# A Fourier and state-space block: which engine makes the second parts of the projection's weights while a context or first latent scan runs

## The chip, the cores and the metric

The kernel runs on one core of a Trainium2 chip, in one launch. The metric is the device time of that launch in microseconds (us), lower is better. Five engines of the core take part, each with its own list of instructions that it works off in order, and each waiting for the others through semaphores:

- TensorE (PE in the profile): matmuls; its weight loads (PEld) overlap them.
- VectorE (DVE), ScalarE (ACT) and GpSimd (POOL): element-wise work.
- SyncE (SP): issues nearly all DMAs. A few are issued by ScalarE.

The engines share an on-chip memory (SBUF). Matmuls write to PSUM, a small second memory, from which VectorE and ScalarE read.

## The reference, cut to what matters

One layer: a normed and modulated input is projected. The projected columns u go through a 2-D Fourier transform. x, B and C go through a row convolution and then a chunked scan in two directions. z is a gate. The context tokens (256) go the same way first, without an output: only their final scan states are kept, and the latent scans (2048 tokens) start from them.

```python
def mixer_inputs(h, w_in, conv_w, conv_b, rows, row_len, full):
    p = h @ (w_in if full else w_in[:, XBC_OFF:])
    ...
    xbc = jax.nn.silu(conv_rows(rest[..., :CONV_DIM], conv_w, conv_b, rows, row_len))
    dt_raw = rest[..., CONV_DIM:]
...
    y_c, hf_c, hb_c = ssd_bidir(xs_c, B_c, C_c, dt_c, dt_bias[l], a_log[l], h0, h0, keep_ctx)
...
    u_f, z_x, xs_x, B_x, C_x, dt_x = mixer_inputs(hx, w_in[l], conv_w[l], conv_b[l], rows, GRID_W, True)
    y_x, _, _ = ssd_bidir(xs_x, B_x, C_x, dt_x, dt_bias[l], a_log[l], hf_c, hb_c, True)
    x = x + gm_x * rms_norm(mixer_output(uf_x, z_x, xs_x, y_x, d_skip[l], g_ssd[l], w_out[l]), g_post_mix[l])
    ...
    x = x + gf_x * rms_norm(swiglu(hx2, w_gate[l], w_up[l], w_down[l]), g_post_ffn[l])
```

The scan's step, for each chunk of 128 tokens, is h = exp(a) h + s, where s is a matmul of B with weighted x.

## The kernel before, in words

**Exact products.** Every large product is made of three fast ones. A float32 operand is split into a first part `hi` (rounded) and a second part `lo` = value - hi; the product is hi·hi + hi·lo + lo·hi. For weights this is `wparts` (L217): the 512 KB block `raw` of 128 columns is loaded by SP, `hi` is a cast on ScalarE, and `lo` a subtraction of two SBUF tiles of 128x1024, by default on VectorE (V), or on the engine that the caller names. `hi` and `lo` have two buffers each; the four `raw` buffers are shared with the blocks `adaw` of the modulation's weights.

**Projection.** The tokens are in three sections: 2 is the context (256 tokens), 0 and 1 are the halves of the latent ones (1024 each). `blocks` (L789 to L801) lists the column blocks in their order. Blocks of section 2 and 0 alternate first, for B and x, and share weights. Then come the four C blocks of section 0, and then section 1: two u, four B, six x, and C and z blocks mixed. A block (`project`, L439) is 16 steps (`project_step`, 8 for each 512 tokens) of three matmuls into PSUM. There are three PSUM places for blocks: two named `mm` and one named `y`. Between, the 24 columns of dt make a section of their own (`dt_section`, L454): matmuls named `w48` or `w`, then a chain of some 25 small VectorE operations on `dtp`, with two sums by matmul (`a<-dtp,kc` and `a<-dtp,ones`), three exponentials and a logarithm on ScalarE.

**After a block** `finish_block` (L1552) starts two chains of work: `split` (L819), which makes `hi` and `lo` of the block after the next, and `column_block` (L576). The latter is, for x, B and C, one ScalarE and six VectorE operations (`acc`, the convolution, reading PSUM), a SiLU on ScalarE, and for x and B transposes by TensorE and a store. The PSUM place is free again when the sixth VectorE operation is done. Blocks of section 0 beside the context have their `lo` on VectorE (`brief`), all others after the first on GpSimd.

**Scans.** `scan_steps` (L655) runs the context's scan (`scan[2]`), then the forward scan over section 0 (`scan[0]`) and over section 1 (`scan[1]`). A chunk is: load x and B rows (`l_x`, `l_b`), weight x on GpSimd (`xd`, which has one buffer), decay the state on GpSimd (`h`), four matmuls `a<-xd,l_b`, and two VectorE additions that free the two small PSUM banks `a`. `scan[2]` has four such steps.

**Section 1's inputs** (`section_chain`): its second half of rows `xt` is squared (ScalarE), scaled by rows (VectorE, `xt<-xt,rq_y`), transposed by TensorE (32 transposes `a<-ident,xt`), modulated (ScalarE, `v`) and split into `actA` hi and lo by VectorE and GpSimd. The second halves of the two u blocks wait for it.

**The Fourier steps** (`fourier_steps`, L709) run beside section 1's blocks, on VectorE above all, and wait where VectorE is planned to be late (`spare`, L686).

**The order.** All this is issued in one order, written by a planner (`Pace`, L72): chains of work are generators; each issued operation is charged an estimated cost on its engine (L142 to L158), and a chain's next step is taken when the planned TensorE time has come to it. So a change of an operation's engine changes the planned times, and with them the order of later instructions on every engine. `ada_steps` (VectorE's `adacc`) fills in where a block is at its sixth step.

After the last projected block come 16 chunks of outputs and the feed-forward network, which is most of the program.

Of the kernel before, what the change touches and what calls it, by code (L numbers as in the profile page):

```python
# [164 lines left out]
def fourier_ssd_block(ctx, tc, a):  # L165
    nc = tc.nc
    pace = Pace()
    V, S, G, T = (Paced(e, n, pace) for e, n in
                  ((nc.vector, "DVE"), (nc.scalar, "ACT"), (nc.gpsimd, "POOL"), (nc.tensor, "PE")))
# [47 lines left out]
    def wparts(raw, shape, engine=V, first=None, pool=wp, tags=("hi", "lo")):  # L217
        hi = pool.tile(shape, F32R, tag=tags[0], name="hi")
        (first.tensor_copy if first else S.copy)(hi, raw)
        lo = pool.tile(shape, F32R, tag=tags[1], name="lo")  # L220
        engine.tensor_tensor(lo, raw, hi.bitcast(F32), op=ALU.subtract)
        return hi, lo
# [353 lines left out]
    def column_block(kind, j, sec, ps, done):  # L576

        n = CTX if sec == 2 else HALF
        row = CTX if sec == 2 else ROW
        res = []  # L580
        if kind == "x":
            yield from conv(ps, n, row, j, res, done)
            yield from to_tokens(res[0], n, xtok_d[sec], j)
        elif kind == "B":
            yield from conv(ps, n, row, XB + j, res, done)
            if sec < 2:
                put(bT_d[sec][j], res[0])
            yield from to_tokens(res[0], n, btok_d[sec], j)
        elif kind == "C":
            yield from conv(ps, n, row, XB + BB + j, res, done)  # L590
            put(cT_d[sec][j], res[0])
        elif kind == "z":
            sz = g_.tile([P, HALF], F32, tag="tok", name="sz")
            S.activation(sz, ps, AF.Silu)
            done()
            put(szT_d[sec][j], sz)
            last_sz[:] = [sz]
        elif kind == "u":
            uf = g_.tile([P, HALF], F32, tag="tok", name="uf")
            S.copy(uf, ps)  # L600
            done()
            put(ufT_d[sec][j], uf)
# [186 lines left out]
    def group(kind, sec):  # L789
        return [(kind, j, sec) for j in range({"z": ZB, "u": 2, "x": XB, "B": BB, "C": CB}[kind])]  # L790
# [3 lines left out]
    blocks = group("z", 0)[:4] + [("dt", 0, 2)]  # L794
# [15 lines left out]
    def shared(bi):  # L810
        return bi > 0 and blocks[bi - 1][0] != "dt" and blocks[bi] == (*blocks[bi - 1][:2], 0) and blocks[bi - 1][2] == 2
# [7 lines left out]
    def split(bi, *engines, **where):  # L819
        if bi < len(blocks) and shared(bi):  # L820
            wq[bi] = wq[bi - 1]
        elif bi in wraw:
            wq[bi] = wparts(wraw.pop(bi), [P, KD, P], *engines, **where)
        yield
# [580 lines left out]
    with tc.manual_schedule(engines=ordered):  # L1405
# [115 lines left out]
        chains, splits, scan, prep1, begun = {}, {}, {}, {}, {}  # L1521
# [4 lines left out]
        def after(bi, n):  # L1526

            i = nth[bi] + n
            return plain[i] if i < len(plain) else nblk
# [24 lines left out]
        def finish_block(bi, ps):  # L1554
            kind, j, sec = blocks[bi]
            live = [chains[b] for b in plain if b in chains and not chains[b].done and (blocks[b][2] == 2) == (sec == 2)]
            pace.drain(*live[:-1])
            two = after(bi, 2)
            brief = two < nblk and any(blocks[b][2] == 2 for b in (after(bi, 1), two))
            splits[two] = pace.start(split(two, *((V, V) if brief and blocks[two][2] != 2 else (V,) if brief else (G,))))  # L1560
            chains[bi] = pace.start(column_block(kind, j, sec, ps.rearrange("p a b -> p (a b)"), lambda: read.add(bi)))

        def late_steps():
# [9 lines left out]
        while bi < nblk:  # L1573
# [17 lines left out]
            if bi == first1:  # L1591
                b1 = after(bi, 1)
                want(after(bi, 3))
                pz = [place(bi), place(b1)]
                pace.drain(splits[b1])
                for i, b in ((0, bi), (0, b1), (1, bi), (1, b1)):
                    if i == 1 and b == bi:
                        pace.drain(prep1[1])
                    for k in range(KD):
                        project_step(pz[b - bi], wq[b], acts[1][i], i, k)  # L1600
                        pace.due()
                    if i == 1:
                        finish_block(b, pz[b - bi])
                fnet = pace.start(when(lambda: settled("u", 1), fourier_steps()))
                late.append(pace.start(when(lambda: fnet.done and ada.done, load_wo(0, "B"))))
                bi += 2
                continue
# [22 lines left out]
            else:  # L1630
                ps = project(bi, wq[bi], acts[sec])
            finish_block(bi, ps)
            if kind == "x" and j == XB - 1:
                scan[sec] = pace.start(when(lambda sec=sec: ready_to_scan(sec), scan_steps(sec)), 8.0)
# [372 lines left out]
```

## Time and profile before

| | |
|---|---|
| runs timed | 2349.7, 2342.34 and 2350.42 us, median 2349.7 |
| the profiled execution | 2342.21 us, of which 2340.4 are its span |
| mean granted TensorE clock | 0.988 |
| first to last move of this change's weights | 291 to 489 us from the span's start |
| last projected block's end | 704 us |

How to read it: a line of a timeline has the start and the duration in us, the engine, the line in the program (nearly all instructions have L143, the helper that issues them), the operation, the tiles out<-in, and in brackets how long the engine stood idle before it and what released it. DVE stands for VectorE, POOL for GpSimd, ACT for ScalarE, and SPq is the queue from which SyncE issues DMAs. Where an operation's duration is longer than that of its equals, it was held up after its start. A window's row has its start and end, its length, the busy time of PE, PEld, DVE, ACT and POOL (each with its count of instructions), then the mean granted clock of TensorE, the share of the DMA engines and GB/s.

### The profile page before, as it was taken

The page shows a single profiled execution, that of the slowest core. Times are in us where ns is not written, and L with a number is a line of the kernel's source. Part 1 is how long each engine was busy: PE and PEld are TensorE (multiplying, and loading weights), DVE is VectorE, ACT ScalarE, POOL GpSimd, SP SyncE. Part 2 cuts the span into 40 slices and gives each one's busy share as a digit, 9 for nine tenths or more (in the row PEclk, how much of TensorE's full clock was granted, in tenths as well). Part 3 has the DMA queues.
Part 4 walks back from the last instruction along what each step waited for, and adds up shares of the span by engine and source line. Part 5 has one row for each costly group of instructions (what it writes and reads, how often), then busy time and mean ns, then how long its engine had stood idle before and what let it go on. Part 6 is the DMA issues. An engine that isn't in the chain of part 4 may idle for free. (4 is left out here: it accounts for less than half of the span.)

```text
span 2340.4 us, 29917 instructions
## 1 busy us (share of the span) xinstructions
PE 2254.8 (96%) x10861; PEld 1850.9 (79%) x10861; DVE 1543.2 (66%) x2248; ACT 1050.4 (45%) x1949; POOL 871.9 (37%) x595
## 2 busy tenths in 40 slices
PE   7999988999999999988999999999999999999998
PEld 3888866878888888866888887788888878888786
DVE  3475667796548888876655556855555565769666
ACT  4433324344347787756433324333333335454444
POOL 2200133522333444434555554355555541500501
PEclk9999999999999999999999999999999999999999
DMA  9354354554767888733333332532333364458343
GB/s 304 115 164 135 104 169 128 183 170 145 262 209 240 256 253 252 239 113 117 113 108 99 104 99 100 166 113 95 108 99 104 109 230 147 152 178 300 90 134 114
DMA packets 261890, 369.77 MB, mean 158 GB/s; under 512 B 16920, under 2 KB 179812, under 8 KB 258927
## 3 DMA queue, kind: packets, MB, share of 16 engines
q1 hardware_dynamic: 232086, 337.08, 45.2%
q10 hardware_dynamic: 29656, 30.78, 3.8%
q8 instruction: 86, 1.41, 0.3%
q14 instruction: 62, 0.50, 0.1%
HBM read 273.09 MB, written 94.72 MB: 157 GB/s over the span
## 5 line engine op out<-in xcount | busy, mean ns | idle before, releaser
L143 PE MATMUL b<-wd,hd 128*128 128x512 f32 x1848 | 423.1, 391 | 4.4 <-ACT hd L143 2.2
L143 PEld LDWEIGHTS b<-wd,hd 128*128 128x128 f32 x1848 | 347.4, 188 | 80.0 <-DVE slot L143 4.1
L143 PE MATMUL mm<-slot,wa 128*128 128x512 f32 x1584 | 378.8, 392 | 10.5 <-ACT sg L143 6.9
L143 PEld LDWEIGHTS mm<-slot,wa 128*128 128x128 f32 x1584 | 297.7, 189 | 75.8 <-ACT sg L143 7.7
L143 PE MATMUL mm<-actC,wa 128*128 128x512 f32 x984 | 241.5, 394 | 7.3 <-DVE u L143 7.2
L143 POOL TENSOR_TENSOR ws<-raw 128x512 f32<-128x512 f32 x88 | 127.2, 1446 | 310.1 <-DMA raw<-in_w_up_dram 116.5
L143 PE MATMUL mm<-actB,wa 128*128 128x512 f32 x1020 | 239.4, 390 | 0.0
L143 PEld LDWEIGHTS mm<-actC,wa 128*128 128x128 f32 x984 | 186.6, 190 | 47.6 <-issue 8.7
L143 POOL TENSOR_TENSOR lo<-raw,hi 128x1024 fp32r<-128x1024 f32 x33 | 80.1, 2428 | 384.9 <-ACT hi L143 374.3
L143 PEld LDWEIGHTS mm<-actB,wa 128*128 128x128 f32 x1020 | 191.2, 188 | 39.6
L143 ACT CAST wa<-ws 128x512 fp32r<-128x512 f32 x176 | 109.1, 621 | 252.2 <-PE mm L143 212.2
L143 DVE TENSOR_TENSOR wa<-ws,wa 128x512 fp32r<-128x512 f32 x176 | 156.0, 888 | 59.0 <-ACT wa L143 56.1
L143 DVE SCALAR_TENSOR_TENSOR acc<-mm,convw,acc 128x1008 f32<-128x1008 f32 (+3 forms) x156 | 161.9, 1040 | 34.3 <-ACT acc L143 31.6
L143 PE MATMUL mm<-actA,hi 128*128 128x512 f32 x512 | 164.8, 402 | 2.9 <-DVE actA L143 2.5
L143 POOL TENSOR_TENSOR rq_y<-rq_ms,mhalf 128x1 f32<-128x1 f32 (+2 forms) x60 | 42.3, 710 | 331.0 <-DVE rq_ms L143 324.1
L143 DVE TENSOR_TENSOR u<-u,mm 128x512 f32<-128x512 f32 x126 | 86.5, 687 | 116.3 <-PE mm L143 116.2
L143 DVE TENSOR_TENSOR wa<-raw,wa 128x512 fp32r<-128x512 f32 x132 | 120.3, 912 | 65.0 <-ACT wa L143 64.6
L143 ACT CAST wa<-raw 128x512 fp32r<-128x512 f32 x132 | 82.3, 624 | 162.2 <-PE mm L143 147.7
L143 ACT ACTIVATE ab<-ab,lda 128x128 f32<-128x128 f32 x384 | 118.8, 390 | 0.4 <-ACT sz L143 0.4
L143 DVE TENSOR_TENSOR hd<-hraw,hd 128x512 fp32r<-128x512 f32 x154 | 110.0, 715 | 6.2 <-ACT hd L143 6.1
L143 PEld LDWEIGHTS mm<-actA,hi 128*128 128x128 f32 x512 | 93.7, 190 | 24.8 <-DVE actA L143 3.2
L143 PE MATMUL mm<-actC,hi 128*128 128x512 f32 (+1 forms) x384 | 108.0, 368 | 0.0
(306 smaller groups left out, 4329.1 us busy)
## 6 DMA issues: line engine op xcount, KB each, us to landing
hraw<-hg SPq DMA_DIRECT2D x70, 512.0 KB
ab<-acsd SPq DMA_DIRECT2D x128, 192.0 KB
raw<-in_w_in_dram SPq DMA_DIRECT2D x44, 512.0 KB
raw<-in_w_gate_dram SPq DMA_DIRECT2D x44, 512.0 KB
raw<-in_w_up_dram SPq DMA_DIRECT2D x44, 512.0 KB
hg<-hs SPq DMA_DIRECT2D x22, 1024.0 KB
adaw<-in_w_ada_dram SPq DMA_DIRECT2D x32, 512.0 KB
l_x<-xtok SPq DMA_DIRECT2D x33, 384.0 KB
```

The costliest lines, as they stand in the source:

```text
L143: r = issue(out, *args, **kw)
```

## The change

```diff
@@ -1557,7 +1557,8 @@
             pace.drain(*live[:-1])
             two = after(bi, 2)
             brief = two < nblk and any(blocks[b][2] == 2 for b in (after(bi, 1), two))
-            splits[two] = pace.start(split(two, *((V, V) if brief and blocks[two][2] != 2 else (V,) if brief else (G,))))
+            busy = any(not scan[k].done for k in scan if k != 1)
+            splits[two] = pace.start(split(two, *((V, V) if brief and blocks[two][2] != 2 else (V,) if brief or busy else (G,))))
             chains[bi] = pace.start(column_block(kind, j, sec, ps.rearrange("p a b -> p (a b)"), lambda: read.add(bi)))
```

`scan[2]` and `scan[0]` are in the list from the time that the last x block of their section is finished in the planner. From then until `scan[0]` is done in the plan, the `lo` of each new block is issued on VectorE. These are eleven: those of C1 to C3 of section 0, and of section 1 both u blocks, all four B blocks and the first two x blocks. On GpSimd eleven rows are gone, on VectorE there are eleven more. No arithmetic changes. The rest of the order moves by the planner, up to the last projected block; behind it nothing does.

The first place is GpSimd's list beside the context's scan, from the `lo` of C2 on (`xd` are the weighted x of the scan's steps, `actC` second parts of section 1's first inputs). Before:

```order
L143 TENSOR_TENSOR rq_y_2402<-rq_ms_2381,mhalf_86 128x4
L143 TENSOR_TENSOR lo_2437<-raw_2334,hi_2435 128x1024
L143 TENSOR_TENSOR xd_2441<-l_x_2390,scs_127 128x768
L143 TENSOR_TENSOR actC_2462<-v_2477,actC_2461 128x512
L143 TENSOR_TENSOR xd_2504<-l_x_2394,scs_127 128x768
L143 TENSOR_TENSOR actC_2462<-v_2511,actC_2461 128x512
L143 TENSOR_TENSOR h_2444<-h_2443,hdec_128 128x768
L143 TENSOR_TENSOR actC_2462<-v_2555,actC_2461 128x512
L143 TENSOR_TENSOR xd_2585<-l_x_2394,scs_127 128x768
L143 TENSOR_TENSOR actC_2462<-v_2592,actC_2461 128x512
L143 TENSOR_TENSOR lo_2624<-raw_2429,hi_2622 128x1024
L143 TENSOR_TENSOR xd_2634<-l_x_2390,scs_127 128x768
```

And now:

```order
L143 TENSOR_TENSOR rq_y_2405<-rq_ms_2381,mhalf_86 128x4
L143 TENSOR_TENSOR xd_2441<-l_x_2390,scs_127 128x768
L143 TENSOR_TENSOR xd_2464<-l_x_2394,scs_127 128x768
L143 TENSOR_TENSOR actC_2472<-v_2487,actC_2471 128x512
L143 TENSOR_TENSOR h_2444<-h_2443,hdec_128 128x768
L143 TENSOR_TENSOR actC_2472<-v_2512,actC_2471 128x512
L143 TENSOR_TENSOR xd_2553<-l_x_2394,scs_127 128x768
L143 TENSOR_TENSOR actC_2472<-v_2570,actC_2471 128x512
L143 TENSOR_TENSOR actC_2472<-v_2591,actC_2471 128x512
L143 TENSOR_TENSOR xd_2604<-l_x_2390,scs_127 128x768
```

The `lo` of C2, ahead of the first `xd`, and that of C3, ahead of the last, are gone; the one of C1, a row above the first list, is gone too.

The second place is VectorE's list at the end of the context's scan (`hc` is the scan's backward state, `acc_2439` the convolution of C0, whose PSUM tile is `mm_2336`, and `acc_2646` or `acc_2647` that of C1, whose tile is `y_2431`; `dtp` is section 0's dt chain). Before:

```order
L143 SCALAR_TENSOR_TENSOR acc_2439<-mm_2336,convw_352,acc_2439 128x16x61
L143 COPY hc_2621<-a_2626 128x384
L143 COPY hc_2621<-a_2630 128x384
L143 TENSOR_TENSOR hc_2621<-hc_2621,a_2637 128x384
L143 TENSOR_TENSOR hc_2621<-hc_2621,a_2641 128x384
L143 SCALAR_TENSOR_TENSOR acc_2647<-y_2431,convw_352,acc_2647 128x16x63
L143 TENSOR_TENSOR dtp_2685<-a_2712,dtb_354 128x192
L143 SCALAR_TENSOR_TENSOR acc_2647<-y_2431,convw_352,acc_2647 128x16x63
```

And now:

```order
L143 TENSOR_TENSOR hc_2595<-hc_2595,a_2632 128x384
L143 TENSOR_TENSOR hc_2595<-hc_2595,a_2636 128x384
L143 TENSOR_TENSOR lo_2644<-raw_2429,hi_2642 128x1024
L143 SCALAR_TENSOR_TENSOR acc_2439<-mm_2336,convw_352,acc_2439 128x16x61
L143 SCALAR_TENSOR_TENSOR acc_2646<-y_2431,convw_352,acc_2646 128x16x63 x2
L143 SCALAR_TENSOR_TENSOR acc_2646<-y_2431,convw_352,acc_2646 128x16x62
L143 TENSOR_TENSOR dtp_2683<-a_2714,dtb_354 128x192
```

The `lo` of C3 has come in, the last operation of C0's convolution is behind the scan's last addition, and three operations of C1's convolution, not one, stand ahead of the first operation of the dt chain.

The third place is TensorE's list where section 0's dt sums are made (`a_2888` or `a_2954`; `mm_2858` is a u block of section 1). Before:

```order
L143 MATMUL mm_2858<-actC_2462,hi_2768 128x512
L143 MATMUL mm_2858<-actC_2461,lo_2770 128x512
L143 MATMUL a_2888<-dtp_2685,kc_83 128x8x12 x2
L143 MATMUL a_2888<-dtp_2685,ones_84 128x192
L143 MATMUL mm_2858<-actC_2461,hi_2768 128x512
L143 MATMUL mm_2858<-actC_2462,hi_2768 128x512
```

And now:

```order
L143 MATMUL a_2944<-ident_81,xt_2776 128x128
L143 MATMUL a_2944<-ident_81,xt_2778 128x128
L143 MATMUL a_2944<-ident_81,xt_2780 128x128
L143 MATMUL a_2944<-ident_81,xt_2782 128x128
L143 MATMUL a_2954<-dtp_2683,kc_83 128x8x12 x2
L143 MATMUL a_2954<-dtp_2683,ones_84 128x192
L143 MATMUL a_2963<-ident_81,xt_2776 128x128
```

The sums have moved from the middle of a block's matmuls to behind the first eight transposes of section 1's second rows. The first step of `scan[0]` (`a<-xd,l_b`), which stood among those transposes, has moved behind section 1's dt matmuls and into its first B block. One of the four groups of Fourier matmuls that stood beside section 1's B blocks now stands beside its second x block.

## The prediction

> **What bounds the kernel now.** I read the page's busy shares and its chain first, then the busy times by stage, then TensorE's waits with the rows behind them.
>
> ```profile
> PE 2254.8 (96%) x10861; PEld 1850.9 (79%) x10861; DVE 1543.2 (66%) x2248; ACT 1050.4 (45%) x1949; POOL 871.9 (37%) x595
> PE 13%; issue 2%; POOL 1%; DVE 1%; ACT 0%; POOLq 0%; DVEq 0%; ACTq 0%
> ```
>
> TensorE is busy for 96% of the span, and the chain that ended last is TensorE's where it could be followed at all. So time is won or lost only where TensorE stands idle or runs at a lower clock. The change moves eleven subtractions between 291 and 489 us, and the order changes up to 704 us. This is the view of busy times by stage for that part:
>
> ```profile
> 300.00:334.00 34.00, 25.66 (x127) 19.76 (x126) 26.23 (x32) 13.28 (x16) 19.85 (x12) 0.96 0.49 157
> 334.00:381.00 47.00, 44.33 (x201) 33.08 (x198) 31.68 (x45) 17.47 (x23) 5.82 (x3) 0.99 0.46 150
> 381.00:397.00 16.00, 9.42 (x43) 6.96 (x41) 12.40 (x19) 9.11 (x11) 7.68 (x6) 0.68 0.18 64
> ...
> 423.00:503.00 80.00, 74.42 (x376) 61.99 (x376) 71.23 (x111) 33.93 (x54) 32.58 (x20) 0.98 0.52 162
> 503.00:700.00 197.00, 195.72 (x976) 165.01 (x975) 124.69 (x169) 80.59 (x122) 65.02 (x35) 1.00 0.65 210
> ```
>
> Length less PE's busy time is TensorE's idle time: 8.3 us (the context's scan), 2.7 (blocks C2 to u), 6.6 (section 1's transposes), 5.6 (beside `scan[0]`) and 1.3, in all 24.5. The clock below 1.00 hides some 6 more (0.04 of 25.7, 0.01 of 44.3, 0.32 of 9.4, 0.02 of 74.4). So about 30 us is the most that any new order could win here. These waits of TensorE matter below:
>
> ```profile
> 326.29 1.46 PE L143 MATMUL a<-xd,l_b 128*128 128x192 f32 x8
> 331.22 2.81 PE L143 MATMUL a<-xd,l_b 128*128 128x192 f32 x8 [3.47 <-POOL xd L143]
> 356.47 0.73 PE L143 MATMUL y<-actA,hi 128*128 128x512 f32 x2 [1.61 <-DVE acc L143]
> 375.68 0.50 PE L143 MATMUL mm<-actC,lo 128*128 128x512 f32 x1 [0.72 <-POOL lo L143]
> 479.36 0.66 PE L143 MATMUL a<-dtp,kc 128*128 128x96 f32 x4 [1.26 <-DVE dtp L143]
> 485.03 1.12 PE L143 MATMUL a<-ident,acc 128*128 128x128 f32 x4 [2.83 <-ACT hdec L143]
> 501.81 1.09 PE L143 MATMUL a<-ident,acc 128*128 128x128 f32 x8 [1.37 <-ACT acc L143]
> ```
>
> Only two name GpSimd: one a `lo` (0.72), one an `xd` (3.47). The rest are VectorE's and ScalarE's doing.
>
> **The price of a moved subtraction.** The same form stands on both engines:
>
> ```profile
> L143 POOL TENSOR_TENSOR lo<-raw,hi x11: 2351/2403/2412, 291.0 to 488.6; 128x1024 fp32r<-128x1024 f32 x11
> L143 DVE TENSOR_TENSOR lo<-raw,hi x11: 1212/1226/1228, 34.7 to 262.9; 128x1024 fp32r<-128x1024 f32 x11
> ```
>
> GpSimd is rid of 11 x 2.40 = 26.4 us, VectorE gets 11 x 1.23 = 13.5. But GpSimd's `lo` already cost VectorE time:
>
> ```profile
> 451.28 2.41 POOL L143 TENSOR_TENSOR lo<-raw,hi 128x1024 fp32r<-128x1024 f32 x1 [3.07 <-ACT hi L143]
> 451.81 2.10 DVE L143 SCALAR_TENSOR_TENSOR dtp<-dtp 128x192 f32<-128x192 f32 x1
> 467.68 2.41 POOL L143 TENSOR_TENSOR lo<-raw,hi 128x1024 fp32r<-128x1024 f32 x1 [1.71 <-ACT hi L143]
> 467.87 3.30 DVE L143 SCALAR_TENSOR_TENSOR adacc<-adaw,ccol,adacc 128x1024 f32<-128x1024 f32 x1
> L143 DVE SCALAR_TENSOR_TENSOR adacc<-adaw,ccol,adacc x28: 1270/1276/3301, 120.0 to 577.0; 128x1024 f32<-128x1024 f32 x28
> L143 DVE SCALAR_TENSOR_TENSOR dtp<-dtp x20: 342/349/2576, 350.0 to 477.1; 128x192 f32<-128x192 f32 x20
> ```
>
> The `adacc` of 467.87 began in GpSimd's `lo` and took 3.30 us where the median is 1.28: it ended 1.1 us after the `lo`, as if it had only then begun. The `dtp` of 451.81 took 2.10 for 0.35, inside the `lo` of 451.28. So a VectorE operation with two SBUF operands stands still while such a GpSimd operation runs; `acc`, with one operand in PSUM, doesn't. These two lost 2.0 and 1.8 us.
>
> The Trainium skill (SBUF — State Buffer, section "SBUF: two separate sides") states this as an exclusive lock: VectorE and GpSimd share a pair of ports, and a VectorE operation with two SBUF inputs and a GpSimd operation that reads SBUF exclude each other for a whole instruction. The rows above agree. By that rule the added subtraction, which has two SBUF inputs, excludes the scan's `xd` and `h` on GpSimd in its turn, which speaks against the change; that is the second rival below.
>
> **The change, part by part.** The times are against the profiled execution's 2342.2 us (span 2340.4, 1.8 around it).
>
> *Context's scan.* The 3.47 us wait had this cause:
>
> ```profile
> 327.38 2.36 POOL L143 TENSOR_TENSOR lo<-raw,hi 128x1024 fp32r<-128x1024 f32 x1 [1.46 <-ACT hi L143]
> 329.69 1.48 POOL L143 TENSOR_TENSOR xd<-l_x,scs 128x768 f32<-128x768 f32 x1
> ```
>
> The last `xd` stood behind C3's `lo`. Now no `lo` stands there, and four transposes and four steps of the block lie between the last two groups of scan matmuls. A step takes 0.68 us by the first two rows below, so that is over 2.7 us, against 1.5 of `xd`. The wait goes: -3.5. The eight matmuls behind it took 2.81 us instead of 1.46, a slow clock after the gap: -1.3. The first scan matmul comes earlier, after the block's fourth step, at 300.1 + 4 x 0.68 = 302.8 us, and may wait for its `xd`, which needs the load:
>
> ```profile
> 300.10 0.62 PE L143 MATMUL y<-actA,hi 128*128 128x512 f32 x2
> 300.78 0.62 PE L143 MATMUL y<-actA,hi 128*128 128x512 f32 x2
> 299.25 0.81 SPq L650 DMA_DIRECT2D l_x<-xtok  x2
> 604.07 0.82 SPq L650 DMA_DIRECT2D l_x<-xtok  x2
> 607.11 1.48 POOL L143 TENSOR_TENSOR xd<-l_x,scs 128x768 f32<-128x768 f32 x1 [0.38 <-DMA l_x<-xtok]
> ```
>
> A load like it was used 3.0 us after its issue (607.11 after 604.07), so `xd` would run from 302.3 to 303.8: a new wait of about 1.1. The other 4.9 us of waits here (transposes paced by `v` and `xt`) are spread better, with block steps between each pair; I take 1.8 of them as gone. The three `lo` here add up to 1.2 us each to VectorE's list; C3's is not used before the dt matmuls and all of C2 are through. Sum -5.5. Bounds: -8.3 - 1.0 (all idle time and clock) and +1.2 (nothing won, one `lo` on the path).
>
> *C2 to u.* The wait at 356.47 was for C1's convolution, held up behind the dt chain's first operation:
>
> ```profile
> 348.55 0.36 DVE L143 TENSOR_TENSOR dtp<-a,dtb 128x192 f32<-128x192 f32 x1 [12.74 <-PE a L143]
> ```
>
> VectorE stood 12.7 us there, with five of the six operations queued behind it. Now three stand ahead, so 2.4 us less is left to do: the 1.61 goes. The wait for a `lo` (0.72) goes as well, and the rest of 0.3 I count with them: -2.7 together, the stage's whole idle time. What is late next are section 1's rows. Here the change adds a wait: u1's `lo` now sits in VectorE's queue behind the last operation of C2's convolution, and its `hi` is behind that convolution's SiLU on ScalarE:
>
> ```profile
> 371.11 1.06 ACT L143 ACTIVATE acc<-acc 128x1024 f32<-128x1024 f32 x1 [8.43 <-DVE acc L143]
> 372.07 1.03 ACT L143 CAST hi<-raw 128x1024 fp32r<-128x1024 f32 x1
> 380.99 1.41 DVE L143 TENSOR_SCALAR xt<-xt,rq_y 128x1024 f32<-128x1024 f32 x2
> 381.79 0.33 PE L143 MATMUL a<-ident,xt 128*128 128x128 f32 x1 [0.56 <-DVE xt L143]
> ```
>
> So VectorE stands about 2 us and then works 1.2, and behind it wait the rest of the dt chain, C3's convolution and the four scalings of `xt`. TensorE already waited for these (0.56), and will come 5.5 + 2.7 = 8.2 us earlier. Bounds 0 and +3.3 (2.1 of standing and 1.2 of work, all of it on the path); I take +2.0, nearer to the upper end, because there was no slack before.
>
> *Transposes.* This stage is a round of TensorE, ScalarE and VectorE: 16 us with 9.4 of matmuls at clock 0.68. The dt sums come into it, and with them a table load and three exponentials of ScalarE:
>
> ```profile
> 375.26 1.28 ACT L143 ACT_TABLE_LOAD   x1
> 376.56 0.33 ACT L143 ACTIVATE hdec<-a 128x192 f32<-128x192 f32 x1
> 393.90 2.64 PE L143 MATMUL a<-xd,l_b 128*128 128x192 f32 x8
> ```
>
> That is 1.28 + 3 x 0.35 = 2.3 us of ScalarE, which paces. A scan step of 2.64 us leaves (it will cost 1.2 later). I take -1.0, with bounds -3 and +2.3. The two `lo` of B0 and B1 come next and fall where VectorE waited 20 us for a scan step, so at nothing; without that cover they would cost 2.5:
>
> ```profile
> 421.12 1.15 DVE L143 TENSOR_TENSOR h<-h,a 128x384 f32<-128x384 f32 x2 [20.04 <-issue]
> ```
>
> *Beside `scan[0]`.* VectorE is busy for 71.2 of 80 us. It gets four `lo` (4.9) and one more scan addition (1.1), is rid of the waits behind GpSimd's `lo` (3.8 in the two shown), and one of four Fourier groups goes later, a quarter of these rows' 14.3 us, 3.6:
>
> ```profile
> L143 DVE TENSOR_TENSOR actB<-va 128x128 f32<-128x128 f32 (+1 forms) x24 | 9.1, 446 | 0.0
> L143 DVE SCALAR_TENSOR_TENSOR actB<-va 128x128 f32<-128x128 f32 x16 | 5.2, 380 | 0.0
> ```
>
> 6.0 come and 7.4 go: nearly even. The TensorE waits here (1.26 + 2.83 + 1.37) belong to the second dt chain, which ends on the same engines in the same kind of order: 0, bounds -7 (all of them and the clock) and +8.
>
> *Up to 704 us.* Fourier work and the output weights come later, beside a stage with 1.3 us of idle time; I put +1.0 for it.
>
> Sum: -5.5 - 2.7 + 2.0 - 1.0 + 0 + 1.0 = -6.2, or 2336.0 us. The three timed runs were 2342.3, 2349.7 and 2350.4, so executions lie at two levels, and the profiled one at the lower. The mean of the four is 2346.2, 4.0 above it; I add 4 and forecast 2340 for the median.
>
> **Rivals.** *The waits beside `scan[0]` and at the transposes go too.* If VectorE is freed there as well, 5.6 us of idle time, 1.5 of clock and 2 of the transposes come on top: -15.3, 2327 + 4 = 2331. For it: a VectorE operation held up for 2 to 3 us lengthens every chain behind it. Against: the dt chain's order stays. *VectorE becomes the bound beside `scan[0]`.* Four `lo` cost 4.9, each may first stand behind a scan operation of 1.48 (5.9), and the added scan step costs 1.1: 11.9, with no hold-up saved because the chain's small operations fall into `xd` and `h` instead. VectorE's idle time there is 80 - 71.2 = 8.8 us, part of it waits for TensorE; where the additions exceed it, a convolution ends late, its PSUM place is not free, and TensorE waits. Costing all 11.9 and 1.5 of clock, less the 6.2: +7.2, 2349 + 4 = 2353. For it: VectorE is busy for 89% of the stage. Against: the hold-ups above go. *Given back.* What is won early is lost at the late waits (second dt chain, the first chunk of outputs): 2342 + 4 = 2346. That the change doesn't do what it says is excluded by the lists of instructions.
>
> **How the numbers follow.** Forecast 0.50, first rival 0.26, second 0.12, third 0.12. About 0.5% (11.7 us) is what a measurement of this kernel can tell from no change. The first rival is beyond it; of the second, half is taken as dearer than worked out and beyond it; a little of the forecast's is beyond too. So faster 0.28, same 0.66, slower 0.06. The range reaches from the first rival's 2331 with its bounds to the second's 2353 and the upper level: 2326 to 2354.
>
> **What would show it.** Right: no `lo` on GpSimd between 290 and 490 us; the last context-scan matmul without a wait over 1 us; no wait for `acc` at C3; the transposes starting 6 to 9 us earlier, after a wait for `xt` of 2 to 3 us; beside `scan[0]` again some 5 us of idle time. Wrong: waits for `acc` at section 1's B or x blocks (the second rival), or a stage from 503 to 700 us with more than 3 us of idle time (the third).

## The result and the profile after

The changed kernel takes 2376.95 us (median of 5, 2375.23 to 2377.62) where the kernel before takes 2349.7 (median of 5, 2342.34 to 2351.4). The ratio is 1.0139, with a 95% interval of 1.0123 to 1.0156: slower by 1.4%. (The ratios are not the quotients of the medians; here that would be 1.0116. The runs of the kernel before lie at two levels, near 2342 and near 2350 us, and its median here falls on the upper one.) The forecast was 2340 with a range of 2326 to 2354. The profiled execution of the changed kernel took 2375.23 us, 33.0 more than that of before.

The view of busy times by stage comes first, for the changed kernel, with the columns of the prediction:

```profile
300.00:334.00 34.00, 30.05 (x147) 20.80 (x146) 28.67 (x36) 12.07 (x15) 15.77 (x10) 0.95 0.53 176
334.00:381.00 47.00, 42.05 (x195) 33.36 (x193) 33.84 (x50) 21.09 (x28) 2.28 (x2) 0.94 0.42 136
381.00:397.00 16.00, 12.61 (x48) 9.98 (x47) 8.38 (x16) 8.57 (x11) 6.90 (x5) 0.65 0.19 65
...
423.00:503.00 80.00, 66.72 (x323) 55.44 (x322) 64.27 (x98) 25.23 (x38) 22.84 (x15) 0.95 0.50 160
503.00:700.00 197.00, 182.36 (x888) 151.78 (x887) 134.09 (x161) 71.58 (x99) 64.40 (x34) 0.96 0.61 192
700.00:900.00 200.00, 192.54 (x1150) 165.44 (x1149) 149.80 (x304) 145.01 (x361) 76.21 (x63) 0.97 0.72 225
```

TensorE's idle time is a row's length less its first busy time. The first three rows together have 12.3 us where there were 17.6 (4.0 for 8.3 in the first; the second has 5.0 for 2.7, because the transposes now begin in it). Then 13.3 us stand beside `scan[0]` (423 to 503) where there were 5.6, 14.6 from 503 to 700 where there were 1.3, and 7.5 from 700 to 900, where before had 0.9 (its row there: 199.07 busy of 200). VectorE, which got four of the subtractions (5.1 us) in the stage beside `scan[0]`, is *less* busy there than before, 64.3 us for 71.2, with 98 operations for 111. Over the stage it is not full; it stands in the wrong places.

The stages don't hold the same work in both kernels, so here is the same thing at equal work: when the n-th matmul of the projection's blocks ended, counted from TensorE's timelines of both kernels.

```
end of                before   after   difference
C1 of section 0        353.9   348.5     -5.4
both u of section 1    407.3   400.4     -6.9
the last B block       480.8   471.3     -9.5
the first x block      499.5   493.6     -5.9
the second x block     512.9   516.0     +3.1
the last x block       567.5   565.5     -2.0
the first C block      579.3   579.1     -0.2
the last C block       654.4   663.4     +9.0
the last z block       704.2   726.5    +22.3
```

Up to the last B block the changed kernel was 9.5 us *ahead*. It lost 12.6 in two x blocks, won some back (Fourier matmuls that before had done by then were still to come), and lost 24 beside the C and z blocks. Of the other 10.7 of the 33.0, 9.7 come within 25 us behind the last block. The last 1.0 is spread over the rest of the program, where the compute engines' lists are the same. This is TensorE's timeline, the rows with the large waits:

```profile
303.62 1.57 PE L143 MATMUL a<-xd,l_b 128*128 128x192 f32 x8 [1.08 <-POOL xd L143]
323.31 0.92 PE L143 MATMUL a<-xd,l_b 128*128 128x192 f32 x4 [0.26 <-ACT v L143]
372.57 0.33 PE L143 MATMUL a<-ident,xt 128*128 128x128 f32 x1 [1.22 <-DVE xt L143]
379.45 3.16 PE L143 MATMUL a<-ident,xt 128*128 128x128 f32 x12 [2.91 <-ACT hdec L143]
477.62 1.97 PE L143 MATMUL a<-ident,acc 128*128 128x128 f32 x8 [5.44 <-ACT acc L143]
501.55 1.97 PE L143 MATMUL a<-ident,acc 128*128 128x128 f32 x8 [6.21 <-ACT acc L143]
613.57 0.79 PE L143 MATMUL mm<-actC,hi 128*128 128x512 f32 x2 [3.98 <-DVE acc L143]
686.69 1.19 PE L143 MATMUL mm<-actC,hi 128*128 128x512 f32 x2 [6.54 <-DVE acc L143]
741.39 1.62 PE L143 MATMUL a<-l_h,l_cT 128*128 128x192 f32 x4 [6.60 <-DVE dg L143]
```

The last five are 28.8 us, and none of them is in the kernel before. Three of them come when all `lo` are back on GpSimd (the first one there starts at 505.7 us). A wait for `acc` says that a convolution was late, but not why. The lists of the engines around the wait at 501.55 say it (TensorE, VectorE, ScalarE in order of time; the last row is the same read in the kernel before):

```profile
493.70 0.58 PE L143 MATMUL a<-dtp,kc 128*128 128x96 f32 x4
494.68 0.36 DVE L143 COPY dtp<-a 128x192 f32<-128x192 f32 x1 [5.92 <-PE a L143]
495.34 5.07 DVE L143 SCALAR_TENSOR_TENSOR acc<-y,convw,acc 128x992 f32<-128x992 f32 x4
500.44 1.06 ACT L143 ACTIVATE acc<-acc 128x1024 f32<-128x1024 f32 x1 [1.51 <-DVE acc L143]
...
482.54 0.34 DVE L143 COPY dtp<-a 128x192 f32<-128x192 f32 x1
```

VectorE stood 5.92 us for the sums of the dt chain, with four operations of a convolution behind that read in its list; in the kernel before it didn't stand there. TensorE made the sums when its own list came to them, had little left to do before the convolution's transposes, and then waited for four operations of 1.25 and a SiLU. Nothing was overloaded here: each engine waited for the other in turn. The wait at 613.57 is of the same kind (VectorE stood 11.69 us at 603.74 for the sums of `adacc`, with a C block's convolution behind them). The wait at 477.62 is of another kind. After a scan step of TensorE VectorE worked for over 8 us without a break, with the last three operations of the B block's convolution spread among a scan addition, the dt chain, Fourier work and `adacc`:

```profile
468.20 1.15 DVE L143 TENSOR_TENSOR h<-h,a 128x384 f32<-128x384 f32 x2 [0.33 <-issue]
476.51 1.06 ACT L143 ACTIVATE acc<-acc 128x1024 f32<-128x1024 f32 x1 [9.10 <-DVE acc L143]
```

The last two come from lists in which a DMA stands ahead (the second row is the group of the four stores, with their shortest, median and longest time in ns and the first and last start):

```profile
665.64 8.40 ACTq L786 DMA_DIRECT2D fT<-fo  x4
L786 ACTq DMA_DIRECT2D fT<-fo x4: 332/618/1159, 665.6 to 673.7; - x4
676.33 1.27 DVE L143 SCALAR_TENSOR_TENSOR acc<-mm,convw,acc 128x1008 f32<-128x1008 f32 x1 [8.53 <-ACT acc L143]
729.44 2.68 SPq L1034 DMA_DIRECT2D ab<-acsd  x4
732.22 0.68 SPq L1022 DMA_DIRECT2D l_sz<-szT  x1
737.97 0.96 DVE L143 TENSOR_TENSOR yg<-y,l_sz 128x768 f32<-128x768 f32 x1 [8.40 <-DMA l_sz<-szT]
```

The four stores of the Fourier result held ScalarE for 8.40 us, and a C block's convolution begins with an operation of ScalarE that stood behind them. Issuing them took only some 2.7 us of this (the four durations added up). The fourth started at 673.7 us, 5.5 us after the third had been issued. By the trace's semaphore events it waited until a load `l_b`, which SyncE had issued at 667.23 us and which uses the same semaphore, had landed at 673.63. Then SyncE, which had issued nothing since 716.67 us, issued four loads `ab` of the next chunk ahead of the gates `l_sz`, and VectorE stood 8.40 us for the gates; in the kernel before they stand ahead of these loads. The Fourier steps end 54 us later than before: their last matmuls start at 663.23 us in the changed kernel and at 608.96 in the one before.

### The profile page after: what moved, and what is told of

Its sections match the earlier page's. It is cut to its first block, busy times and chain, and to the rows that moved or that the text cites. A ratio compares the mean times of both kernels' runs of the same rounds, so it can differ in the third digit from the quotient of the medians.

```text
span 2373.4 us, 29920 instructions
## 1 busy us (share of the span) xinstructions
PE 2262.9 (95%) x10861; PEld 1857.1 (78%) x10861; DVE 1563.5 (66%) x2259; ACT 1051.5 (44%) x1950; POOL 849.3 (36%) x584
## 5 line engine op out<-in xcount | busy, mean ns | idle before, releaser
L143 POOL TENSOR_TENSOR lo<-raw,hi 128x1024 fp32r<-128x1024 f32 x22 | 53.2, 2418 | 331.7 <-ACT hi L143 320.5
```

What stands on the lines that cost most here:

```text
L143: r = issue(out, *args, **kw)
```

## The experiments

Two theories at first. ORDER: the subtraction is cheap on VectorE, and the planner's new order makes the loss. ENGINE: VectorE has too much to do beside `scan[0]`, and all else follows. The planner charges a `lo` to the engine that it is given, so the two can be taken apart: `Paced` takes an engine and a name under which its work is charged. All times are medians; the kernel before ran beside every kernel and its medians there are 2342.7 to 2343.2.

**Engine without order.** `lo` on VectorE, charged to GpSimd.

```diff
+    VP = Paced(nc.vector, "POOL", pace)
...
+            busy = any(not scan[k].done for k in scan if k != 1)
-   ... else (V,) if brief else (G,)
+   ... else (V,) if brief else (VP,) if busy else (G,)
```

> The eleven subtractions run on VectorE, but the planner charges them to GpSimd at GpSimd's cost, so that every engine's list is that of before with those rows moved. Theory ORDER (the loss of 27 us comes from what the planner rearranged, above all the Fourier steps and what hangs on their end; the subtraction itself is cheap on VectorE): 2335 to 2352 us, none of the waits of 6 us at 686 and 741 us of the changed kernel. Theory ENGINE (VectorE has too much to do beside the first latent scan, the convolutions end late there, and all later waits follow from that): 2365 us or more, with waits for acc of 5 us between 420 and 520 us.

Measured: 2343.3, ratio 0.9997 (0.9987 to 1.0007). ENGINE falls. In this order the rule moves ten subtractions, not eleven; but for these rows every compute engine's list is that of the kernel before. None of the waits of 6 us at 686 and 741 us is there, but the early gain isn't either: TensorE stands 8.3 us from 300 to 334 us, as before. VectorE's, GpSimd's and TensorE's rows at the end of the context's scan:

```profile
331.06 2.46 DVE L143 TENSOR_TENSOR lo<-raw,hi 128x1024 fp32r<-128x1024 f32 x1
333.44 1.01 DVE L143 COPY hc<-a 128x384 f32<-128x384 f32 x2
330.96 1.47 POOL L143 TENSOR_TENSOR xd<-l_x,scs 128x768 f32<-128x768 f32 x1 [1.98 <-PE a L143]
334.13 2.90 PE L143 MATMUL a<-xd,l_b 128*128 128x192 f32 x8 [3.31 <-DVE hc L143]
```

The `lo` of C3 no longer stands ahead of the last `xd`. It now stands on VectorE ahead of the two copies `hc<-a` that free the scan's PSUM banks, and takes 2.46 us where its equals take 1.23, as it began while the `xd` ran. The last scan matmuls wait 3.31 us, where they waited 3.47 in the kernel before.

**Order without engine.** The mirror: `lo` on GpSimd, charged to VectorE.

```diff
+    GD = Paced(nc.gpsimd, "DVE", pace)
...
+   ... else (V,) if brief else (GD,) if busy else (G,)
```

> The mirror of the run before it: the subtractions stay on GpSimd, but the planner charges them to VectorE at VectorE's cost, so that every engine's list is that of the changed kernel with those rows moved back. Theory ORDER: 2365 to 2385 us, with the waits at 614, 687 and 741 us as in the changed kernel. Theory ENGINE: 2340 to 2352 us.

Measured: 2375.8, ratio 1.0130 (1.0112 to 1.0149): the whole loss, without one subtraction moved. TensorE's timeline of this run has the waits of the changed kernel, some to a hundredth:

```profile
480.81 1.97 PE L143 MATMUL a<-ident,acc 128*128 128x128 f32 x8 [5.44 <-ACT acc L143]
504.75 1.97 PE L143 MATMUL a<-ident,acc 128*128 128x128 f32 x8 [6.22 <-ACT acc L143]
690.24 1.19 PE L143 MATMUL mm<-actC,hi 128*128 128x512 f32 x2 [6.74 <-DVE acc L143]
```

That a wait doesn't change when 1.2 us of VectorE's work are taken from ahead of it fits the reading above, that it is counted from TensorE's own last result. This order, with the `lo` on GpSimd, also has no wait at the last scan matmuls, and 5.3 us of idle time from 300 to 334 us: most of the early gain is the order's too.

**Parts.** `busy` for one scan alone.

```diff
+            busy = 2 in scan and not scan[2].done
...
+            busy = 0 in scan and not scan[0].done and scan[2].done
```

> Only the subtractions that are planned while the context's scan runs (C1 to C3 of section 0) go to VectorE. Theory ENGINE: no loss, 2338 to 2350 us, since nothing is added beside the first latent scan. Theory ORDER gives no size for a new order: it says only that any loss stands at waits on chains that the planner moved, and that the stage from 300 to 334 us gains 4 us as in the changed kernel.

Measured: 2346.1, ratio 1.0001 (0.9989 to 1.0013), as both theories allow. The stage from 300 to 334 us has 3.9 us of idle time.

> Only the subtractions that are planned while the first latent scan runs go to VectorE. Theory ENGINE: the whole loss, 2370 to 2385 us, with waits for acc of 5 us beside that scan. Theory ORDER: a loss or none according to where the Fourier steps end; if they end at 611 us as before, within 8 us of before, if at 650 us or later as in the changed kernel, 2360 us or more.

Measured: 2358.6, ratio 1.0059 (1.0036 to 1.0082). Its Fourier steps end at 663 us, as ORDER asked for a loss; 2358.6 is a little under the 2360 that it said. It is far from ENGINE's 2370 to 2385, and the largest wait for `acc` beside the scan is 3.12 us and not 5.

**Which part of the order?** A `lo` on VectorE changes two planned times: VectorE's is later, GpSimd's earlier. Charged to no engine, it leaves VectorE's as it was:

```diff
+    VN = SimpleNamespace(tensor_tensor=nc.vector.tensor_tensor)
...
+   ... else (V,) if brief else (VN,) if busy else (G,)
```

> The eleven subtractions run on VectorE as in the changed kernel, but the planner charges them to no engine: GpSimd's planned time is as free as in the changed kernel, VectorE's as free as in the kernel before. Theory PLANNED VECTORE (the loss comes from VectorE's planned time being 11 x 1.13 us later, which puts the Fourier steps and the convolutions' operations later in the lists): 2338 to 2355 us, no waits of 4 us or more between 600 and 760 us. Theory PLANNED GPSIMD (it comes from the chains that follow GpSimd's earlier planned time): 2365 us or more, with those waits.

Measured: 2333.2, ratio 0.9943 (0.9922 to 0.9964): faster than both kernels. So the loss comes from VectorE's planned lateness. (Nine subtractions are moved in this order.) The same order with the subtractions on GpSimd (`nc.gpsimd.tensor_tensor`, uncharged) shows how much of this gain is the order's:

> The order of the uncharged run with the eleven subtractions on GpSimd and not on VectorE (every other row the same). If its gain of 10 us is the order's alone, 2331 to 2338 us; if it needs the subtractions on VectorE, 2340 us or more.

Measured: 2336.6, ratio 0.9962 (0.9948 to 0.9977). Most of the gain is the order's. The two medians are 3.4 us apart, but the intervals of their ratios overlap, so it is not shown that the subtractions on VectorE add to it.

**What waits for a planned VectorE?** The Fourier steps do, by a rule of their own (`spare`, L689): they hold while VectorE is planned to be over 1.2 us late. One number, in the kernel before and in the changed one:

```diff
-        while not (pace.hurry or pace.forced) and pace.busy["DVE"] > pace.now + 1.2:
+        while not (pace.hurry or pace.forced) and pace.busy["DVE"] > pace.now + 0.9:
...
+        while not (pace.hurry or pace.forced) and pace.busy["DVE"] > pace.now + 0.0:
```

> The kernel before with nothing moved to VectorE; only the Fourier steps wait for a VectorE that is planned less than 0.9 us late, where they take 1.2. By the lists their last group of matmuls then stands 32 us of TensorE work later, near where the changed kernel has it. Theory FOURIER (their late end is what makes the waits after 600 us, 17 us of them): 2355 to 2368 us, with waits of 4 us or more between 600 and 760 us. Rival (they only went late beside the real cause): 2340 to 2351 us.

Measured (0.9, kernel before): 2350.1, ratio 1.0023 (1.0010 to 1.0037). Slower, but this is a miss for FOURIER: 2350.1 lies in the range of its rival, and no wait reaches 4 us. The new waits for `acc` are small, though they stand where that theory has them, at C blocks:

```profile
606.57 0.73 PE L143 MATMUL mm<-actC,hi 128*128 128x512 f32 x2 [1.68 <-DVE acc L143]
667.80 0.81 PE L143 MATMUL mm<-actC,hi 128*128 128x512 f32 x2 [1.89 <-DVE acc L143]
```

> The changed kernel, with the Fourier steps waiting for a VectorE that is planned to be not late at all; by the lists their last group of matmuls stands 29 us of TensorE work earlier than in the changed kernel, near where the kernel before has it. Theory FOURIER: the three waits after 600 us go, those for acc at 478 and 502 us stay: 2353 to 2365 us. Rival (bystander): 2368 us or more, with waits of 4 us or more after 600 us.

Measured (0.0, changed kernel): 2340.7, ratio 0.9978 (0.9965 to 0.9991). The whole loss is gone, 36 us, for a change of one number in the rule for the Fourier steps, with every `lo` still on VectorE and charged there. Up to 430 us its waits are those of the changed kernel. More went than either theory said (2353 to 2365, or 2368 and more): the waits at 478 and 502 us went too (0.50 and 0.32 us are left, at 474 and 494). The number doesn't act as its meaning suggests: a stricter limit brought the steps *earlier* here and later in the run before it. The planner's response is not smooth.

**Is it the dt chain?** In the slow orders the sums of section 1's dt chain also stood late. So this was a theory (LATE DT), tried from both sides: the chain's seven operations without a break, in the changed kernel, and a delay ahead of the sums, in the kernel before.

```diff
-            yield
+            if m == 3 or sec != 1:
+                yield
...
-        yield
+        yield 11.0 if sec == 1 else None
```

> The changed kernel, with the seven operations of the series in section 1's dt chain issued without a break between them, so that the chain's sums come earlier in the lists (in the last B block and no longer in the first x block), while the Fourier steps end as late as in the changed kernel. Theory LATE DT (what separates the slow orders from the fast ones is that section 1's dt chain stands late in VectorE's list, where convolutions are queued behind its reads of TensorE's sums): 2340 to 2358 us, TensorE's waits at 478 and 502 us gone, the later ones at most 8 us in all. Rival (the late Fourier steps do it): 2365 us or more.

Measured: 2353.6, ratio 1.0032 (1.0019 to 1.0046). The wait at 502 is gone, that at 482 us is not (4.79), and one of 5.82 at 674 us is there.

> The kernel before, with nothing moved to VectorE, and a delay of 11 us planned ahead of the sums of section 1's dt chain, so that they stand in the first x block as in the changed kernel; the Fourier steps end some 19 us later in the plan than before, 15 us earlier than in the changed kernel. Theory LATE DT: 2355 us or more, with waits of TensorE for acc or hdec of 4 us or more between 470 and 525 us. Rival: 2341 to 2351 us.

Measured: 2356.9, ratio 1.0048 (1.0034 to 1.0062). The times went as LATE DT said, though the second run's largest wait for `acc` is 3.62 us and not 4; but on the chip the Fourier steps ended late in both (646 and 642 us). The case that tells the two apart has the dt delay and the Fourier steps early, in the changed kernel (both edits, 11.0 and 0.0):

> The changed kernel with the Fourier steps early (as in the run that was at 2341 us), and a delay of 11 us planned ahead of the sums of section 1's dt chain, which brings them into the first x block. Theory LATE DT: 2352 us or more, with waits of TensorE for acc of 3 us or more between 460 and 530 us. Rival LATE FOURIER (the dt chain's place costs nothing of its own, only the late Fourier steps do): 2336 to 2347 us.

Measured: 2343.5, ratio 0.9994 (0.9982 to 1.0006), with the sums at 483 us, in the first x block as planned. There is no wait for `acc` of over 1 us between 460 and 530 us. LATE DT falls as a cause of its own. The one large wait is a new one:

```profile
608.45 2.93 PE L143 MATMUL a<-xd,l_b 128*128 128x192 f32 x8 [7.43 <-POOL xd L143]
```

**Two of the waits by themselves.** The stores of the Fourier result through SyncE (L786, `put` becomes `dma`); no list of a compute engine changes but for these four rows, while SyncE's own list moves in a few more places:

> The changed kernel, with the four stores of the Fourier result issued by SyncE and no longer by ScalarE; no compute engine's list changes otherwise. If TensorE's wait of 6.5 us at 687 us comes from ScalarE standing 7.9 us behind these stores with a convolution's first operation queued behind them, that wait is under 1 us and the time 2368 to 2372 us. If it has another cause, the wait and 2374 to 2379 us stay.

Measured: 2366.7, ratio 1.0087 (1.0061 to 1.0112), 10.3 us less than the changed kernel, and more than the 5 to 9 expected. The wait is 1.53 us where it was 6.54 (rows below), and not under 1; the granted clock from 503 to 700 us is 0.99 where it was 0.96:

```profile
670.39 1.27 DVE L143 SCALAR_TENSOR_TENSOR acc<-mm,convw,acc 128x1008 f32<-128x1008 f32 x1 [2.13 <-ACT acc L143]
682.13 0.70 PE L143 MATMUL mm<-actC,hi 128*128 128x512 f32 x2 [1.53 <-DVE acc L143]
```

And one convolution operation ahead of the dt sums' reads:

```diff
         T.matmul(ps[:, n24 : 2 * n24], ones, da, start=True, stop=True)
+        if sec == 1:
+            yield 0.1
```

> The changed kernel, with VectorE's two reads of the dt sums planned 0.1 us later. Up to the wait at 502 us TensorE's and VectorE's lists are those of the changed kernel, but for one of the four convolution operations that stand behind these reads and now stands ahead of them. If TensorE's wait of 6.2 us there is made of these operations, one after another, it shrinks by one of them, 1.25 us, to 4.9 to 5.1 us. If the exponentials on ScalarE or the transposes' own place set it, it stays at 6.0 to 6.3 us. The lists differ a little at the first chunk of outputs, so the time of the whole is not predicted beyond 2368 to 2380 us.

Measured: 2373.3, ratio 1.0126 (1.0107 to 1.0145). The wait is 4.93 us where it was 6.21, less by 1.28, which is one operation. VectorE's and TensorE's rows:

```profile
495.73 0.36 DVE L143 COPY dtp<-a 128x192 f32<-128x192 f32 x1 [4.76 <-PE a L143]
496.40 3.78 DVE L143 SCALAR_TENSOR_TENSOR acc<-y,convw,acc 128x992 f32<-128x992 f32 x3
501.32 1.97 PE L143 MATMUL a<-ident,acc 128*128 128x128 f32 x8 [4.93 <-ACT acc L143]
```

All runs side by side, in the order of the Fourier steps' end (the start of their last matmuls in the profiled execution), with the start of section 1's dt sums and TensorE's idle time from 503 to 700 us:

| kernel | `lo` on | Fourier's end | dt sums | idle 503 to 700 | median | ratio |
|---|---|---|---|---|---|---|
| dt late, Fourier early | VectorE | 586 | 483 | 7.4 | 2343.5 | 0.9994 |
| context part | part | 589 | 485 | 3.0 | 2346.1 | 1.0001 |
| uncharged | VectorE | 608 | 477 | 0.5 | 2333.2 | 0.9943 |
| before | GpSimd | 609 | 479 | 1.3 | 2342.7 to 2343.2 | |
| uncharged, GpSimd | GpSimd | 611 | 480 | 0.5 | 2336.6 | 0.9962 |
| Fourier early | VectorE | 613 | 469 | 2.4 | 2340.7 | 0.9978 |
| engine only | VectorE | 615 | 488 | 2.6 | 2343.3 | 0.9997 |
| dt late | GpSimd | 642 | 496 | 10.7 | 2356.9 | 1.0048 |
| Fourier late | GpSimd | 645 | 474 | 9.0 | 2350.1 | 1.0023 |
| dt early | VectorE | 646 | 459 | 7.1 | 2353.6 | 1.0032 |
| changed | VectorE | 663 | 494 | 14.6 | 2377.0 | 1.0139 |
| `scan[0]` part | part | 663 | 506 | 8.2 | 2358.6 | 1.0059 |
| stores on SyncE | VectorE | 664 | 494 | 9.7 | 2366.7 | 1.0087 |
| one op ahead | VectorE | 665 | 495 | 14.3 | 2373.3 | 1.0126 |
| order only | GpSimd | 667 | 497 | 16.8 | 2375.8 | 1.0130 |

Which engine runs the `lo` does not decide the time. Every order whose Fourier steps end by 615 us is as fast as before or faster; every one in which they end at 642 or later is slower, by 0.2 to 1.4%. So it is shown that the new order makes the loss, and that it comes in through VectorE's planned lateness. That the late Fourier steps are what costs the time is the reading that fits all these orders best, but it is not shown: each edit also rewrites the rest of the order, no run moves the Fourier steps and nothing else, and the run that delayed them in the kernel before lost only 7 us. How much a late end goes with, 7 us or 34, is the sum of single waits like those above, and differs from order to order.

**What stays open.** Why the waits at 478 and 502 us went together with the late Fourier steps is not settled. The wait at 741 us is read from SyncE's list only; it was not tried apart.

## Why the prediction was wrong

- *Context's scan, -5.5.* Right in size: -5.4 at the end of C1, the first scan matmul after a wait of 1.08 us for `xd` (forecast 1.1), and no wait of over 1 us at the last one. The cause that it names first is not enough, though. In the engine-only run no `lo` stands ahead of the last `xd`, and the last scan matmuls still wait 3.31 us. It is the other thing named, the transposes and block steps that the new order puts between the last two groups, that goes with the wait's end: the order-only run has these, and no wait there. In part this term was right by luck.
- *C2 to u and the wait for `xt` rows, -2.7 and +2.0; transposes, -1.0.* Right in their sum: with the first term -7.2 forecast, -6.9 measured at the end of both u. The transposes start 9.2 us earlier (372.57 for 381.79) after waits of 1.22 and 0.33; I had said 6 to 9 after 2 to 3.
- *VectorE's account beside `scan[0]`.* Right in kind: much of what the subtractions cost came back through shorter operations, how much depends on the order (next section but one).
- *Beside `scan[0]`: 0.* Wrong. The step says that the waits there "belong to the second dt chain, which ends on the same engines in the same kind of order". It did not: before, VectorE did not stand at its read of the sums; in the changed order it stood 5.92 us there, with four operations of a convolution behind it. Idle time rose by 7.7 us (13.3 for 5.6), near the upper bound of +8, with clock lost besides (0.95 for 0.98).
- *Up to 704 us: +1.0.* This is the step that failed most. I put +1.0 for late Fourier work beside a stage with 1.3 us of idle time, with no row behind it and no upper bound. A stage without idle time shows that *this* order has no waits there, not that another one will have none. From the end of the last x block to the last z block the changed kernel lost 24.3 us (from 2.0 ahead to 22.3 behind), with waits of 3.98 and 6.54 us for `acc`.
- *Nothing behind 704 us.* Wrong by 9.7 us, all within 25 us behind the last block: the compute engines' lists are the same there, but SyncE's is not, and I did not cost its list.
- *Second rival* (VectorE the bound, waits for `acc` at B or x blocks). Its waits came, 5.44 and 6.21 us; its cause, the added work, did not: the order-only run has the same waits with the `lo` on GpSimd. The Trainium skill's rule on the shared ports (SBUF — State Buffer, section "SBUF: two separate sides") made a rival of the added subtractions. The engine-only run agrees with the rule in one place, where a `lo` took 2.46 us beside an `xd`; the time of the whole didn't change (0.9997).
- *Third rival* (given back late, at the second dt chain and the first chunk of outputs). Right in its places, and much too small: it was priced at what had been won, 6 us, and a new order can lose what it never won.
- The 4.0 us that I added for the median: in later comparisons before ran at both levels again, more often at the lower, with medians 0.5 to 1.0 us above 2342.2.

## What to carry to other kernels

Where a planner writes the order, a change of one operation's engine is two changes: test them apart, by charging the work to the engine that it left. Cost the reordering as a term of its own, with a range taken from what other orders of the same kernel do (here from -10 to +34 us), and not from the idle time of the order that was tuned. When a wait names a slow engine, look what stands ahead in that engine's list before calling it full: in four of the five large waits here it was a read of TensorE's result or a DMA, with the work that TensorE needed queued behind. At the fifth VectorE was busy, with that work spread among other chains' operations.

## What the runs showed of the hardware beyond that

VectorE gets back a part of the time of a subtraction that it takes over from GpSimd. These are VectorE's busy time from 285 to 520 us (third busy time of the row) and two of its groups, of the kernel before:

```profile
285.00:520.00 235.00, 211.68 (x1009) 167.33 (x1008) 172.69 (x248) 96.42 (x136) 85.74 (x50) 0.96 0.49 157
L143 DVE SCALAR_TENSOR_TENSOR adacc<-adaw,ccol,adacc 128x1024 f32<-128x1024 f32 x11 | 18.7, 1701 | 0.0
L143 DVE SCALAR_TENSOR_TENSOR dtp<-dtp 128x192 f32<-128x192 f32 x20 | 11.9, 595 | 0.2
```

And the same of the engine-only run, which has the same lists but for the ten moved rows:

```profile
285.00:520.00 235.00, 211.32 (x983) 167.29 (x982) 172.19 (x249) 92.19 (x128) 60.04 (x39) 0.93 0.47 154
L143 DVE TENSOR_TENSOR lo<-raw,hi 128x1024 fp32r<-128x1024 f32 x10 | 13.5, 1346 | 14.8 <-ACT hi L143 14.8
L143 DVE SCALAR_TENSOR_TENSOR adacc<-adaw,ccol,adacc 128x1024 f32<-128x1024 f32 x10 | 12.7, 1271 | 0.0
L143 DVE SCALAR_TENSOR_TENSOR dtp<-dtp 128x192 f32<-128x192 f32 x20 | 8.5, 424 | 0.2
```

VectorE did 13.5 us of subtractions more in this stretch and was busy for 172.2 us in place of 172.7. The second stretch holds a little less work, however: ten rows have come in, and the count has risen by one only, so nine other operations fall outside. What can be compared is the time of one operation. `adacc` took 1.27 us on the mean where it had taken 1.70, the small `dtp` 0.42 for 0.60. For these two groups that is 4.3 and 3.4 us, which fits the two operations that the prediction's rows show standing still beside GpSimd's subtractions. Over all groups, each with as many operations as both stretches have, it comes to some 8 us of the 13.5 (an estimate from the means).

How much comes back depends on the order. Between the order-only run and the changed kernel, which differ in nothing but the engine, the same estimate up to the last projected block gives some 5 us of 13.7; between the two uncharged runs some 3 of 11.0. By this the Trainium skill's rule on the shared ports (SBUF — State Buffer, section "SBUF: two separate sides") is borne out, and what it is worth in a stage can be told only from the list that runs there. As TensorE waited for little of it, the kernel was not faster for it.
